# RWKV heads: step outputs formed inside the chain, gathers of the next pair through the levels' banks and ScalarE, ahead of the inversion

## The chip, the cores and the metric

The kernel runs on one core of one Trainium2 chip. The metric is the device time of one execution in microseconds (us); lower is better. The engines of a core are named as in the profile: PE (TensorE; PEld is its weight load), DVE (VectorE), ACT (ScalarE), POOL (GpSimd) and SP (SyncE). PSUM, where PE writes its results, has 8 banks.

## The reference, cut to what matters

The network is two blocks. The first normalises, projects, runs two recurrent mixers side by side (a gated delta rule and RWKV-7) and projects out; the second is banded attention with a conformer convolution. The change touches only the RWKV mixer, which per direction and head is this recurrence over 256 context and 512 latent tokens:

```python
def rwkv7_scan(r, w, k, v, kk, b_vec, s0):
    def step(state, inp):
        r_t, w_t, k_t, v_t, kk_t, b_t = inp
        sa = -jnp.einsum('bhvk,bhk->bhv', state, kk_t)
        state = (state * w_t[:, :, None, :] + sa[..., None] * b_t[:, :, None, :]
                 + v_t[..., None] * k_t[:, :, None, :])
        return state, jnp.einsum('bhvk,bhk->bhv', state, r_t)
    ...

def rwkv_output(o, bonus, z, gn_g, gn_b):
    ...
    y = ((o - mu) * lax.rsqrt(var + GN_EPS)).reshape(b, n, D_RWKV) * gn_g + gn_b
    y = (y + bonus.reshape(b, n, D_RWKV)) * jax.nn.silu(z.astype(jnp.float32))
```

There are 16 heads of 64 channels and two directions; only the outputs of the 512 latent tokens are needed in the end. The two mixers' outputs go through one projection, x + gate * (concat(ya, yb) @ w_out).

## The kernel before, in words

The recurrence is computed in chunks. The 768 tokens are 12 chunks of 64 (4 of context, 8 latent); two heads make a pair, so there are 8 pairs, one after the other, each with both directions at once. For a pair p the stages are these:

- `rwkv_keys(p)` (L932) and in it `rwkv_prep`: loads k and r, forms the decays, A (row operands, rows 12 to 19 of it for the latent outputs) and BK (key operands). `gram` multiplies BK with A on PE into tile `rpg`, and DVE masks it into `Ga` (L1067).
- `rwkv_lanes(p)` (L1072): the inversion of the 64x64 triangles of `Ga`, cut into 32x32 blocks. DVE transposes the blocks into `rL` (L1080), runs 60 operations in a row (`lanes_solve`, L745 and L746, 30 each, tiles `rT` and `rL`), and transposes back.
- `rwkv_rest(p)` (L1091): the second gram, into `Gr` (the masks are DVE again, L1067); copies `R` and the transposes `rpt` that become `bk`; then the gathers for the chain: values (`rpv`, ScalarE copies into `UV`, L1126 and L1127), A transposed (`rat`, L1132, copied into `UV` by DVE, L1133), and Ga times values (`rgv`, L1137, copied into `GS` by ScalarE, L1139). There are 6 each of `rpv`, `rat` and `rgv` in a pair.
- `rwkv_levels(p)` (L1148): puts the 32x32 inverses together (`rpy`, `rpx`), then applies them to what the gathers brought (`rmx`).
- `rwkv_chain(p)` (L1175): the 12 steps that follow one another. A step multiplies Ga with GS (`pU`, L1184), ScalarE copies the result into `UV` (L1186), PE adds the state and bk times UV in the other half of the same bank (L93 is the helper that accumulates), and DVE scales it into the next `GS` (L1195). That last operation is called the state update; there are 11.
- `rwkv_o(p)`: 64 matmuls, after the whole chain, form the outputs from all 12 `UV` and `GS` in tile `rpo`.
- `rwkv_out(p)` (L971): group norm on DVE, transposes back on PE (`rpto`, L993), bonus and gate on GpSimd, and a DMA to `y_scr`.

The banks of PSUM in this phase are four pairs: tag "g" (grams, gathers, prep), tag "l" (the levels), tag "pU" (chain, outputs, output transposes) and "mm" for the filler. `A`, `BK`, `Gr`, `bk`, `R` and `Ga` have two buffers, `UV`, `GS`, `rL` and `rT` one.

What order the instructions stand in is decided by a scheduler that takes what is ready by priority. The work of the pairs stands under `tc.high_priority(offset=4000)`. Beside it runs filler of low priority: large matmuls (`mm`, three products of split operands for each tile) that project the inputs of pair p+2 (`rwkv_proj`, L394) and, once there is none left, the first 13 of 16 rows of the output projection (`out_cols`, L1323). With the latter run the sums for the gates, `awt`: weights are loaded and summed up by DVE (L1254). Filler is paced: each `tick(step, n)` in the pair's work makes n slots behind its last matmul, and `Stream` lets the next filler instruction be issued only after its slot. A pair makes 280 slots.

The order of the calls for a pair is short enough to show:

```python
rwkv_rest(p, now)
nxt = rwkv_keys(p + 1) if p + 1 < npairs else None
rwkv_levels(p, now)
rwkv_chain(p, now)
if nxt:
    rwkv_lanes(p + 1, nxt)
rwkv_o(p, now)
rwkv_out(p, now)
```

Of the kernel before, what the change touches and what calls it, by code (L numbers as in the profile page):

```python
# [10 lines left out]
FT = mybir.dt.float32  # L11
# [7 lines left out]
P = 128  # L19
# [185 lines left out]
def build(tc, a, dbg=None):  # L205
# [5 lines left out]
    with root:  # L211
# [717 lines left out]
        def pg_(shape, name):  # L929
            return gps.tile(shape, FT, name=name, tag="g", bufs=2)  # L930
# [160 lines left out]
        def rwkv_rest(p, s):  # L1091
# [21 lines left out]
            for d in dirs:  # L1113
                rv = (lambda t: t[:, :, ::-1]) if d else (lambda t: t)
                vr = vv
                if d:
                    vr = t3("vr")
                    S.activation(rv(ck(vr)), ck(vv), AF.Copy)
                v00 = rp.tile([P, P], FT, name="v00", tag="wup", bufs=2)
                G.tensor_copy(v00.rearrange("p (o t) -> p o t", o=2), vr[:, 0:64].rearrange("p (o t) -> p o t", o=1).to_broadcast([P, 2, 64]))  # L1120
                for i0 in range(0, NC, 4):
                    pt = pg_([P, 4, P], "rpv")
                    for i in range(4):
                        c = step_chunk[d][i0 + i]
                        w2 = vr[:, 64 * (c - 1):64 * (c + 1)] if c else v00
                        PE.transpose(pt[:, i, :], w2, ident)  # L1126
                    S.activation(UV[64:, i0:i0 + 4, d].rearrange("p i h t -> p i (h t)"), pt[64:], AF.Copy)  # L1127
                for c0 in range(0, NC, 4):
                    i0 = step_chunk[d].index(c0 + (3 if d else 0))
                    pt = pg_([P, 4, P], "rat")  # L1130
                    for c in range(4):
                        PE.transpose(pt[0:64, c, :], A[d][:, c0 + c], ident)  # L1132
                    V.tensor_copy(UV[0:64, c0:c0 + 4, d].rearrange("p c h t -> p c (h t)"), pt[0:64])  # L1133
                    pt = pg_([P, 4, 2, 64], "rgv")
                    for i in range(4):
                        for h in range(2):
                            PE.matmul(pt[halves[h], i, h, :], Ga[64:, d, step_chunk[d][i0 + i], h], UV[64:, i0 + i, d, h, :], start=True, stop=True, skip_group_check=True)  # L1137
                    for h, hp_ in enumerate(halves):
                        S.activation(GS[0:64, i0:i0 + 4, d, h], pt[hp_, :, h], AF.Copy)  # L1139
# [34 lines left out]

        def rwkv_chain(p, s):  # L1175
            mark(f"r{p} chain")
            Ga, UV, GS, bk, WC = (s[n] for n in ("Ga", "UV", "GS", "bk", "WC"))
            flat = lambda t: t.rearrange("p d h t -> p (d h t)")
            for i in range(NC):
                pU = cps.tile([P, 2, 2, 64], FT, name="pU", tag="pU")  # L1180
                for d in dirs:
                    for h in range(2):
                        ks = slice(0, P if i else 64)
                        step = PE.matmul(pU[0:64, d, h], Ga[ks, d, step_chunk[d][i], h], GS[ks, i, d, h], start=True, stop=True, skip_group_check=True)  # L1184
                tick(step, 4)
                S.activation(UV[0:64, i], pU[0:64], AF.Copy)  # L1186
                if i < NC - 1:
                    acc = Acc(tc)
                    if i:
# [4 lines left out]
                    tick(step, 4)  # L1194
                    state = V.tensor_tensor(GS[64:, i + 1], pU[64:], WC[64:, i].rearrange("p d (h o) -> p d h o", o=1).to_broadcast([64, 2, 2, 64]), op=OP.mult)  # L1195
                    states.append(state.ins)

        def rwkv_o(p, s):
            mark(f"r{p} o")
            Gr, R, UV, GS = (s[n] for n in ("Gr", "R", "UV", "GS"))  # L1200

            po = cps.tile([P, 4, 2, 64], FT, name="rpo", tag="pU")
            acc = Acc(tc)
            for part in range(2):
                for d in dirs:
                    for h in range(2):
                        for c in range(4, NC):
                            i = step_chunk[d].index(c)
                            dst = po[halves[c % 2], c // 2 - 2, h]
                            if part == 0:  # L1210
                                step = acc(dst, Gr[d][:, c - 4, h], UV[:, i, d, h, :])
                            else:
                                step = acc(dst, R[d][64:, h, c - 4], GS[64:, i, d, h])
                            if c % 4 == 3:
                                tick(step, 2)
            s["po"] = po

        npairs = {"rwkv": 2}.get(dbg, 8)

# [2 lines left out]
        def tick(step, n):  # L1222

            credit[0] += n
            while credit[0] >= 1:
                slots.append(step.ins)
                credit[0] -= 1
# [55 lines left out]
            rwkv_proj(p, r0, False, pace, tag="mix", bufs=2)  # L1283
        with tc.high_priority(offset=4000):
            now = rwkv_keys(0)
            rwkv_lanes(0, now)
        for p in range(npairs):
            start.append(len(slots))
            with tc.high_priority(offset=4000):
                rwkv_rest(p, now)  # L1290
                nxt = rwkv_keys(p + 1) if p + 1 < npairs else None
                rwkv_levels(p, now)
                rwkv_chain(p, now)
                if nxt:
                    rwkv_lanes(p + 1, nxt)
                rwkv_o(p, now)
                rwkv_out(p, now)
                now = nxt
            beside = Beside()
# [490 lines left out]
```

## Time and profile before

| what | value |
| --- | --- |
| time, median of 3 runs | 3431.95 us (3423.43 to 3436.43) |
| the profiled execution | 3426.15 us, span 3424.3 us |
| granted clock of PE, mean | 0.91 of full |
| PE busy | 3107.4 us, 91% of the span |
| PEld busy | 2464.2 us, 72% |
| DVE busy | 2342.5 us, 68% |
| ACT busy | 1277.3 us, 37% |
| POOL busy | 953.5 us, 28% |

The profile is of one execution. Its span is the time between the first and the last instruction recorded. Busy time is a share of the whole; since the program has stages with different limits, the rows further down are for stretches of it. The pairs' chains lie between about 1300 and 2490 us. The granted clock is the share of full speed that the chip allowed PE; its two levels are 1.2 and 2.4 GHz, and a mean between 0.5 and 1 is a mixture of them. In rows on operations, `out<-in` names the tiles, `x` is a count, and a bracket behind a row holds the idle time of the engine ahead of it and what ended that.

### The profile page before, as it was taken

The page shows a single profiled execution, that of the slowest core. Times are in us where ns is not written, and L with a number is a line of the kernel's source. Part 1 is how long each engine was busy: PE and PEld are TensorE (multiplying, and loading weights), DVE is VectorE, ACT ScalarE, POOL GpSimd, SP SyncE. Part 2 cuts the span into 40 slices and gives each one's busy share as a digit, 9 for nine tenths or more (in the row PEclk, how much of TensorE's full clock was granted, in tenths as well). Part 3 has the DMA queues.
Part 4 walks back from the last instruction along what each step waited for, and adds up shares of the span by engine and source line. Part 5 has one row for each costly group of instructions (what it writes and reads, how often), then busy time and mean ns, then how long its engine had stood idle before and what let it go on. Part 6 is the DMA issues. An engine that isn't in the chain of part 4 may idle for free. (4 is left out here: it accounts for less than half of the span.)

```text
span 3424.3 us, 53583 instructions
## 1 busy us (share of the span) xinstructions
PE 3107.4 (91%) x20464; PEld 2464.2 (72%) x20464; DVE 2342.5 (68%) x4044; ACT 1277.3 (37%) x2719; POOL 953.5 (28%) x794
## 2 busy tenths in 40 slices
PE   7898898999898979999899988898968999999996
PEld 4487787788776767767677766676656778877775
DVE  7977768876786264555636478979358997573577
ACT  4133443344433333334333333331323336574423
POOL 3644344334442323233232325231042000002001
PEclk9899999999998978899798987888878999999998
DMA  8522222222212311112121236575143322223764
GB/s 327 194 75 80 78 78 64 67 78 78 72 63 78 100 56 53 61 57 69 45 73 57 70 91 208 182 234 183 41 164 127 120 86 87 87 80 117 253 214 135
DMA packets 206267, 375.14 MB, mean 110 GB/s; under 512 B 21912, under 2 KB 52281, under 8 KB 202681
## 3 DMA queue, kind: packets, MB, share of 16 engines
q1 hardware_dynamic: 196384, 356.07, 32.4%
q10 hardware_dynamic: 9624, 15.64, 1.3%
q8 instruction: 160, 2.62, 0.3%
q14 instruction: 99, 0.80, 0.1%
HBM read 333.75 MB, written 37.88 MB: 109 GB/s over the span
## 5 line engine op out<-in xcount | busy, mean ns | idle before, releaser
L275 POOL TENSOR_TENSOR w_l<-w_f,w_h 128x512 fp32r<-128x512 f32 x380 | 532.5, 1403 | 1058.5 <-ACT w_h L274 972.2
L274 ACT ACTIVATE w_h<-w_f 128x512 fp32r<-128x512 f32 (+2 forms) x688 | 424.3, 618 | 808.7 <-PE mm L394 277.1
L394 PE MATMUL mm<-hxh,w_h 128*128 128x512 f32 x1472 | 619.9, 421 | 11.9 <-ACT w_h L274 10.8
L394 PE MATMUL mm<-hxh,w_l 128*128 128x512 f32 x1472 | 619.1, 421 | 8.9 <-DVE w_l L275 4.9
L394 PE MATMUL mm<-hxl,w_h 128*128 128x512 f32 x1472 | 609.3, 414 | 0.0
L394 PEld LDWEIGHTS mm<-hxh,w_h 128*128 128x128 f32 x1472 | 289.6, 197 | 73.6 <-ACT w_h L274 13.8
L394 PEld LDWEIGHTS mm<-hxh,w_l 128*128 128x128 f32 x1472 | 291.0, 198 | 70.6 <-DVE w_l L275 9.2
L394 PEld LDWEIGHTS mm<-hxl,w_h 128*128 128x128 f32 x1472 | 290.2, 197 | 61.1 <-issue 1.2
L275 DVE TENSOR_TENSOR w_l<-w_f,w_h 128x512 fp32r<-128x512 f32 (+2 forms) x308 | 219.9, 716 | 142.7 <-ACT w_h L274 140.9
L1254 DVE SCALAR_TENSOR_TENSOR awt<-awt,cacts 128x512 f32<-128x512 f32 x180 | 168.5, 936 | 18.0 <-DMA awt<-in_w_ada 13.5
L1499 DVE SCALAR_TENSOR_TENSOR uc<-up,vecs,uc 128x512 f32<-128x512 f32 x240 | 169.6, 751 | 2.2 <-ACT uc L1497 1.0
L1065 PEld LDWEIGHTS rpg<-A,BK 64*128 64x128 f32 x1280 | 133.3, 229 | 29.5 <-issue 9.9
L394 PE MATMUL mm<-hch,w_l 128*128 128x256 f32 x512 | 153.0, 299 | 1.4 <-POOL w_l L275 1.3
L1065 PE MATMUL rpg<-A,BK 64*128 64x64 f32 x1280 | 142.2, 319 | 13.2 <-POOL BK L1051 6.8
L394 PE MATMUL mm<-hch,w_h 128*128 128x256 f32 x512 | 149.7, 293 | 0.0
L394 PE MATMUL mm<-hcl,w_h 128*128 128x256 f32 x512 | 147.4, 288 | 0.0
L745 DVE TENSOR_TENSOR DG<-L 128x30 f32<-128x30 f32 (+14 forms) x240 | 135.8, 566 | 5.4
L746 DVE TENSOR_TENSOR L<-L,DG 128x30 f32<-128x30 f32 (+14 forms) x240 | 133.7, 557 | 5.4
L1195 DVE TENSOR_TENSOR GS<-pU,WC 64x256 f32<-64x256 f32 x88 | 37.6, 428 | 136.2 <-PE pU L93 131.4
L236 POOL TENSOR_TENSOR cv<-cv,mh 128x4 f32<-128x4 f32 x1 | 1.4, 1437 | 436.8 <-DVE cv L1567 436.8
L745 DVE TENSOR_TENSOR rT<-rL 128x30 f32<-128x30 f32 (+14 forms) x240 | 118.9, 495 | 6.1
L746 DVE TENSOR_TENSOR rL<-rL,rT 128x30 f32<-128x30 f32 (+14 forms) x240 | 116.7, 486 | 6.1
(483 smaller groups left out, 6772.1 us busy)
## 6 DMA issues: line engine op xcount, KB each, us to landing
w_f<-in_w_in SPq DMA_DIRECT2D x496, 256.0 KB, 3.0
awt<-in_w_ada SPq DMA_DIRECT2D x192, 256.0 KB, 3.3
wt<-in_w_ada_t SPq DMA_DIRECT2D x20, 1024.0 KB, 7.1
w_f<-in_w_out SPq DMA_DIRECT2D x80, 256.0 KB, 3.1
awt<-in_w_ada_g SPq DMA_DIRECT2D x64, 256.0 KB, 3.2
wk<-in_w_ada_s SPq DMA_DIRECT2D x16, 768.0 KB, 6.5
w_f<-in_w_out_a SPq DMA_DIRECT2D x48, 256.0 KB, 3.2
lth<-lora_scr SPq DMA_DIRECT2D x32, 288.0 KB, 3.7
```

The costliest lines, as they stand in the source:

```text
L236: G.tensor_tensor(out, in_, mh[:in_.shape[0]].to_broadcast([in_.shape[0], n]), op=OP.pow)
L274: S.activation(wh, raw, AF.Copy)
L275: lower[0].tensor_tensor(wl, raw, wh, op=OP.subtract)
L394: PE.matmul(po[:, :n], w_[:, k, :], h_, start=(kt == 0 and i == 0), stop=(kt == KT - 1 and i == 2))
L745: V.tensor_tensor(t, U[:, r, k:k + 1].to_broadcast([n, k, nc_]), U[:, k:k + 1, c].to_broadcast([n, k, nc_]), op=OP.mult)
L746: step = V.tensor_tensor(U[:, r, c], U[:, r, c], t, op=OP.add)
L1065: ticks[p, d, "gram"] = PE.matmul(pg[h][:, c], BK[hp_, c0 + c, :, :], cols[hp_, c], start=True, stop=True, skip_group_check=True).ins
L1195: state = V.tensor_tensor(GS[64:, i + 1], pU[64:], WC[64:, i].rearrange("p d (h o) -> p d h o", o=1).to_broadcast([64, 2, 2, 64]), op=OP.mult)
L1254: V.scalar_tensor_tensor(wt, wt, cvec[:, k:k + 1], acc, op0=OP.mult, op1=OP.add)
L1499: V.scalar_tensor_tensor(uc[t], up[:, j:j + NX], cw(j), uc[t], op0=OP.mult, op1=OP.add)
```

## The change

Three things are changed in the RWKV part. Line numbers after it shift a little: the chain's `pU` is L1201 and its state update L1214.

1. The gathers. Tiles `rat` and `rgv` are taken from the levels' tag "l" instead of "g", and the copy of `rat` into `UV` is ScalarE's instead of DVE's.
2. The outputs. `rwkv_o` is gone. `outputs(i)` forms what step i adds to the outputs; it is called in step i+1 behind the copy of `UV`, and once after the loop. Its tile `rpo` comes from tag "l" rather than "pU". The tick behind the `pU` matmuls makes 3 slots instead of 4, and the ticks of `rwkv_o` are gone, so that a pair has 236 slots.
3. The inversion of a pair is called after its own `rwkv_rest` and ahead of the next pair's `rwkv_keys`, and no longer behind the chain of the pair before.

```diff
--- before.py
+++ after.py
@@ -1127,11 +1127,11 @@
                     S.activation(UV[64:, i0:i0 + 4, d].rearrange("p i h t -> p i (h t)"), pt[64:], AF.Copy)
                 for c0 in range(0, NC, 4):
                     i0 = step_chunk[d].index(c0 + (3 if d else 0))
-                    pt = pg_([P, 4, P], "rat")
+                    pt = gps.tile([P, 4, P], FT, name="rat", tag="l")
                     for c in range(4):
                         PE.transpose(pt[0:64, c, :], A[d][:, c0 + c], ident)
-                    V.tensor_copy(UV[0:64, c0:c0 + 4, d].rearrange("p c h t -> p c (h t)"), pt[0:64])
-                    pt = pg_([P, 4, 2, 64], "rgv")
+                    S.activation(UV[0:64, c0:c0 + 4, d].rearrange("p c h t -> p c (h t)"), pt[0:64], AF.Copy)
+                    pt = gps.tile([P, 4, 2, 64], FT, name="rgv", tag="l")
                     for i in range(4):
                         for h in range(2):
                             PE.matmul(pt[halves[h], i, h, :], Ga[64:, d, step_chunk[d][i0 + i], h], UV[64:, i0 + i, d, h, :], start=True, stop=True, skip_group_check=True)
@@ -1174,16 +1174,35 @@
 
         def rwkv_chain(p, s):
             mark(f"r{p} chain")
-            Ga, UV, GS, bk, WC = (s[n] for n in ("Ga", "UV", "GS", "bk", "WC"))
+            Ga, UV, GS, bk, WC, Gr, R = (s[n] for n in ("Ga", "UV", "GS", "bk", "WC", "Gr", "R"))
             flat = lambda t: t.rearrange("p d h t -> p (d h t)")
+
+            po = s["po"] = gps.tile([P, 4, 2, 64], FT, name="rpo", tag="l")
+            oacc = Acc(tc)
+
+            def outputs(i):
+
+                for part in range(2):
+                    for d in dirs:
+                        c = step_chunk[d][i]
+                        if c < 4:
+                            continue
+                        for h in range(2):
+                            dst = po[halves[c % 2], c // 2 - 2, h]
+                            if part == 0:
+                                oacc(dst, R[d][64:, h, c - 4], GS[64:, i, d, h])
+                            else:
+                                oacc(dst, Gr[d][:, c - 4, h], UV[:, i, d, h, :])
             for i in range(NC):
                 pU = cps.tile([P, 2, 2, 64], FT, name="pU", tag="pU")
                 for d in dirs:
                     for h in range(2):
                         ks = slice(0, P if i else 64)
                         step = PE.matmul(pU[0:64, d, h], Ga[ks, d, step_chunk[d][i], h], GS[ks, i, d, h], start=True, stop=True, skip_group_check=True)
-                tick(step, 4)
+                tick(step, 3)
                 S.activation(UV[0:64, i], pU[0:64], AF.Copy)
+                if i:
+                    outputs(i - 1)
                 if i < NC - 1:
                     acc = Acc(tc)
                     if i:
@@ -1194,26 +1213,7 @@
                     tick(step, 4)
                     state = V.tensor_tensor(GS[64:, i + 1], pU[64:], WC[64:, i].rearrange("p d (h o) -> p d h o", o=1).to_broadcast([64, 2, 2, 64]), op=OP.mult)
                     states.append(state.ins)
-
-        def rwkv_o(p, s):
-            mark(f"r{p} o")
-            Gr, R, UV, GS = (s[n] for n in ("Gr", "R", "UV", "GS"))
-
-            po = cps.tile([P, 4, 2, 64], FT, name="rpo", tag="pU")
-            acc = Acc(tc)
-            for part in range(2):
-                for d in dirs:
-                    for h in range(2):
-                        for c in range(4, NC):
-                            i = step_chunk[d].index(c)
-                            dst = po[halves[c % 2], c // 2 - 2, h]
-                            if part == 0:
-                                step = acc(dst, Gr[d][:, c - 4, h], UV[:, i, d, h, :])
-                            else:
-                                step = acc(dst, R[d][64:, h, c - 4], GS[64:, i, d, h])
-                            if c % 4 == 3:
-                                tick(step, 2)
-            s["po"] = po
+            outputs(NC - 1)
 
         npairs = {"rwkv": 2}.get(dbg, 8)
 
@@ -1283,17 +1283,14 @@
             rwkv_proj(p, r0, False, pace, tag="mix", bufs=2)
         with tc.high_priority(offset=4000):
             now = rwkv_keys(0)
-            rwkv_lanes(0, now)
         for p in range(npairs):
             start.append(len(slots))
             with tc.high_priority(offset=4000):
                 rwkv_rest(p, now)
+                rwkv_lanes(p, now)
                 nxt = rwkv_keys(p + 1) if p + 1 < npairs else None
                 rwkv_levels(p, now)
                 rwkv_chain(p, now)
-                if nxt:
-                    rwkv_lanes(p + 1, nxt)
-                rwkv_o(p, now)
                 rwkv_out(p, now)
                 now = nxt
             beside = Beside()
```

How the scheduler then orders the instructions is shown in three places. The first is DVE at the end of the third pair's chain, before: `GS<-pU,WC` is a state update, `rL<-Ga` the first transposes of the fourth pair's inversion, `rT`/`rL` its operations, and `mr` belongs to filler.

```order
L1195 TENSOR_TENSOR GS<-pU,WC 64x256 x3
L1141 SCALAR_TENSOR_TENSOR ksum<-rmix,vecs_r,ksum 128x512
L1067 TENSOR_TENSOR Ga<-rpg,consts_r 128x8x64 x2
L1195 TENSOR_TENSOR GS<-pU,WC 64x256
L1080 STREAM_TRANSPOSE rL<-Ga 32x1024 x2
L425 SCALAR_TENSOR_TENSOR mr<-mm,vecs,mr 128x8x63
L1067 TENSOR_TENSOR Ga<-rpg,consts_r 128x4x64 x2
L1080 STREAM_TRANSPOSE rL<-Ga 32x1024 x2
L745 TENSOR_TENSOR rT<-rL 128x30
L746 TENSOR_TENSOR rL<-rL,rT 128x30
L745 TENSOR_TENSOR rT<-rL 128x58
L746 TENSOR_TENSOR rL<-rL,rT 128x29x2
```

And in the changed kernel, where `GS<-pU,WC` is L1214 and six of the eleven updates of this chain stand ahead of these rows:

```order
L1214 TENSOR_TENSOR GS<-pU,WC 64x256
L1067 TENSOR_TENSOR Ga<-rpg,consts_r 128x4x64
L1080 STREAM_TRANSPOSE rL<-Ga 32x1024 x2
L425 SCALAR_TENSOR_TENSOR mv<-mm,vecs,mv 32x448 x2
L425 SCALAR_TENSOR_TENSOR mv<-mm,vecs,mv 64x448
L745 TENSOR_TENSOR rT<-rL 128x30
L746 TENSOR_TENSOR rL<-rL,rT 128x30
L745 TENSOR_TENSOR rT<-rL 128x58
L746 TENSOR_TENSOR rL<-rL,rT 128x29x2
L745 TENSOR_TENSOR rT<-rL 128x84
L746 TENSOR_TENSOR rL<-rL,rT 128x28x3
L745 TENSOR_TENSOR rT<-rL 128x108
```

Before, the last update of the chain stands ahead of all transposes and operations of the inversion. In the changed kernel the transposes stand behind the sixth update, and the next updates stand between the inversion's operations.

The second place is PE, one step of the same chain, before: `mm` is filler, `pU<-GS,consts` adds the state.

```order
L394 MATMUL mm<-hxh_85,w_h 128x512
L394 MATMUL mm<-hxh_85,w_l 128x512
L1184 MATMUL pU<-GS,Ga 64x64 x4
L394 MATMUL mm<-hxl_1050,w_h 128x512
L394 MATMUL mm<-hxh_86,w_h 128x512
L394 MATMUL mm<-hxh_86,w_l 128x512
L394 MATMUL mm<-hxl_1100,w_h 128x512
L93 MATMUL pU<-GS,consts 64x256
L93 MATMUL pU<-UV,bk 64x64 x4
L394 MATMUL mm<-hxh_87,w_h 128x512
L394 MATMUL mm<-hxh_87,w_l 128x512
L394 MATMUL mm<-hxl_1177,w_h 128x512
```

And in the changed kernel:

```order
L394 MATMUL mm<-hxh_79,w_l 128x512
L394 MATMUL mm<-hxl_743,w_h 128x512
L1201 MATMUL pU<-GS,Ga 64x64 x4
L93 MATMUL rpo<-GS,R 64x64 x4
L394 MATMUL mm<-hxh_80,w_h 128x512
L394 MATMUL mm<-hxh_80,w_l 128x512
L394 MATMUL mm<-hxl_788,w_h 128x512
L93 MATMUL pU<-GS,consts 64x256
L93 MATMUL pU<-UV,bk 64x64 x4
L93 MATMUL rpo<-UV,Gr 64x64 x4
L394 MATMUL mm<-hxh_81,w_h 128x512
L394 MATMUL mm<-hxh_81,w_l 128x512
```

The eight output matmuls of the step before stand in two groups of four, behind `pU<-GS,Ga` and behind `pU<-UV,bk`, and one filler less stands in the step.

The third place is PE at the gathers of the fourth pair, before; `rpx` and `rpy` are its levels:

```order
L394 MATMUL mm<-hxh_86,w_h 128x512
L394 MATMUL mm<-hxh_86,w_l 128x512
L394 MATMUL mm<-hxl_1100,w_h 128x512
L394 MATMUL mm<-hxh_87,w_h 128x512
L1132 MATMUL rat<-consts,A 64x128 x4
L1160 MATMUL rpx<-Ga,rL 32x32 x6
L1137 MATMUL rgv<-UV,Ga 64x64 x8
L1160 MATMUL rpx<-Ga,rL 32x32 x9
L1132 MATMUL rat<-consts,A 64x128 x4
L1160 MATMUL rpx<-Ga,rL 32x32
L1155 MATMUL rpy<-rL,Ga 32x32 x16
```

And in the changed kernel, between the third pair's chain and the fourth pair's levels; `rbo` is the bonus:

```order
L394 MATMUL mm<-hxh_78,w_h 128x512
L394 MATMUL mm<-hxh_78,w_l 128x512
L394 MATMUL mm<-hxl_666,w_h 128x512
L1126 MATMUL rpv<-consts,v_15484 128x128
L1126 MATMUL rpv<-consts,vmix 128x128 x11
L1137 MATMUL rgv<-UV,Ga 64x64 x8
L1132 MATMUL rat<-consts,A 64x128 x4
L1126 MATMUL rpv<-consts,vr 128x128 x3
L1126 MATMUL rpv<-consts,v_15557 128x128
L1126 MATMUL rpv<-consts,vr 128x128 x4
L1137 MATMUL rgv<-UV,Ga 64x64 x8
L1132 MATMUL rat<-consts,A 64x128 x4
```

Before, `rat` and `rgv` stand among the levels' matmuls and filler. Now they alternate in a row with `rpv`, ahead of the levels, with no filler between them.

## Rows read from the trace of the kernel before

**Rows 1.** Table of stretches of the span: busy time, clock and DMA

```profile
core 0: us, PE busy (x) PEld busy (x) DVE busy (x) ACT busy (x) POOL busy (x), PEclk, DMA share, GB/s
1308.00:2048.00 740.00, 696.19 (x5997) 531.90 (x5999) 410.41 (x677) 268.10 (x504) 218.22 (x157) 0.88 0.21 63
1598.00:1662.00 64.00, 62.67 (x479) 43.75 (x473) 29.11 (x43) 26.80 (x52) 28.24 (x20) 1.00 0.25 75
1662.00:1744.00 82.00, 74.20 (x713) 60.99 (x713) 50.23 (x96) 26.21 (x49) 11.79 (x9) 0.73 0.16 46
1664.00:1698.00 34.00, 29.93 (x213) 25.87 (x213) 32.17 (x65) 4.90 (x8) 0.00 (x0) 0.50 0.06 16
2048.00:2265.00 217.00, 187.57 (x1357) 142.57 (x1355) 187.56 (x261) 73.58 (x139) 82.43 (x58) 0.77 0.65 202
2265.00:2441.00 176.00, 161.45 (x1297) 124.37 (x1294) 135.19 (x218) 55.13 (x108) 33.43 (x25) 0.90 0.53 166
2441.00:2509.00 68.00, 44.97 (x400) 32.05 (x398) 11.87 (x27) 9.60 (x23) 4.16 (x3) 0.63 0.15 47
```

**Rows 2.** Waits of PE, 1308 to 2048 us: total, count, longest

```profile
PE rpt L1105 <- DVE Gr L1067: 15.1, 5, 4.2
...
PE rpy L1155 <- DVE rL L1084: 5.1, 2, 4.3
```

**Rows 3.** Waits of PE, 2048 to 2509 us

```profile
PE pU L1184 <- DVE GS L1195: 26.5, 18, 4.2
```

**Rows 4.** Groups by line: count | busy us, mean ns | idle before, its causes

```profile
L93 PE MATMUL rpo<-GS,R 64*64 64x64 f32 x512 | 30.4, 269 | 0.0
...
L93 PE MATMUL rpo<-UV,Gr 128*64 128x64 f32 x512 | 25.4, 257 | 0.0
...
L745 DVE TENSOR_TENSOR rT<-rL 128x30 f32<-128x30 f32 (+14 forms) x240 | 118.9, 495 | 6.1
L746 DVE TENSOR_TENSOR rL<-rL,rT 128x30 f32<-128x30 f32 (+14 forms) x240 | 116.7, 486 | 6.1
...
L1133 DVE COPY UV<-rat 64x512 f32<-64x512 f32 x48 | 32.6, 678 | 74.0 <-PE rat L1132 74.0
...
L1127 ACT ACTIVATE UV<-rpv 64x512 f32<-64x512 f32 x48 | 27.7, 591 | 20.2 <-PE rpv L1126 15.2 <-DMA awt<-in_w_ada 4.5
...
L1139 ACT ACTIVATE GS<-rgv 64x256 f32<-64x256 f32 x96 | 36.4, 379 | 51.4 <-PE rgv L1137 50.6
...
L1254 DVE SCALAR_TENSOR_TENSOR awt<-awt,cacts 128x512 f32<-128x512 f32 x180 | 168.5, 936 | 18.0 <-DMA awt<-in_w_ada 13.5 <-DMA awt<-in_w_ada_g 1.7
...
L1195 DVE TENSOR_TENSOR GS<-pU,WC 64x256 f32<-64x256 f32 x88 | 37.6, 428 | 136.2 <-PE pU L93 131.4 <-ACT w_h L274 3.1 <-ACT hxh L1312 0.7
```

**Rows 5.** Timeline of ACT, two steps in a chain: start us, us, instruction

```profile
1618.32 0.38 ACT L1186 ACTIVATE UV<-pU 64x256 f32<-64x256 f32 x1 [0.17 <-PE pU L1184]
...
1622.35 0.38 ACT L1186 ACTIVATE UV<-pU 64x256 f32<-64x256 f32 x1 [2.23 <-PE pU L1184]
```

**Rows 6.** Timeline of PE, two fills in a row

```profile
2214.45 0.40 PE L1323 MATMUL mm<-hxh,w_h 128*128 128x512 f32 x1
2214.69 0.39 PE L1323 MATMUL mm<-hxh,w_l 128*128 128x512 f32 x1
```

**Rows 7.** Timeline of DVE, inversion's start and end, last rat copy

```profile
1658.53 3.90 DVE L1080 STREAM_TRANSPOSE rL<-Ga 32x1024 f32<-32x1024 f32 x2
...
1703.23 0.70 DVE L1089 STREAM_TRANSPOSE rT<-rT 32x512 f32<-32x512 f32 x1
...
1738.65 0.68 DVE L1133 COPY UV<-rat 64x512 f32<-64x512 f32 x1 [2.41 <-PE rat L1132]
```

**Rows 8.** Timeline of DVE and POOL, two steps of an inversion

```profile
1542.01 1.62 DVE L745 TENSOR_TENSOR rT<-rL 128x240 f32<-128x240 f32 x1
1543.67 0.57 DVE L746 TENSOR_TENSOR rL<-rL,rT 128x240 f32<-128x240 f32 x1
...
1540.11 3.10 POOL L275 TENSOR_TENSOR w_l<-w_f,w_h 128x512 fp32r<-128x512 f32 x2
```

**Rows 9.** Timeline of PE, the first large matmul behind the last chain

```profile
2509.25 0.80 PE L1323 MATMUL po<-hxh,w_h 128*128 128x512 f32 x1 [7.34 <-ACT hxh L1312]
```

## The prediction

> **What bounds the kernel now.** I read the table of stretches first, then the waits of TensorE (PE), then the timelines at the edges of a chain. The eight pairs of heads run one after another: a chain of 12 steps, then the inversion and the levels of the next pair, then its chain. Five such periods lie between 1308 and 2048 us, 148 us each [rows 1]. In them PE is busy 696.2 of 740 us: 43.8 us idle, under 9 per period. Its mean granted clock there is 0.88, so 0.12 x 2 of the time, 178 us, ran at the lower of the two levels (1.2 instead of 2.4 GHz). In one period the reader is to see two halves: the chain, 64 us at clock 1.00, and the 82 us up to the next chain at 0.73, with 34 us at 0.50 while VectorE (DVE), busy 32 of them, runs the inversion. So PE starves and slows at the inversion; the chain is fed well. What PE waits for in the five periods is mostly the masks of Gr, queued on DVE among the inversion's steps (15.1 us), and the inversion itself (5.1) [rows 2].
> The last 461 us (2048 to 2509) differ: PE idles 67 us, the clock is 0.77, 0.90 and 0.63 in its three rows, and the last chain has no filler: it and the way from it to the next large matmuls take 68 us, with PE busy 45 [rows 1]. Here the chain's state update comes late, 26.5 us in 18 waits [rows 3], behind the awt sums, which fill DVE (187.6 of 217 us).
>
> **Outputs inside the chain.** The 64 output matmuls of a pair (512 records of each kind over 8 pairs) occupy PE (30.4 + 25.4) / 8 = 7.0 us per pair [rows 4], before and after. A clean step lasts 4.03 us [rows 5] with eight fills in it. A fill follows its predecessor by 0.23 us at the full clock [rows 6], so in each step the eight output matmuls (0.9 us) replace one fill: +0.7 us in 8 or 9 steps, taken from the stage after the chain. Sum: 0. What hides the short ScalarE and DVE waits within a step stays: three or four fills and four output matmuls on each side.
>
> **Fewer slots.** Each tick sets where a filler matmul may stand. With the output stage's ticks gone and three instead of four on half of the chain's, the filler is spread further: in the order, 1055 fillers stand between the ends of the first and the sixth pair's mx stage before, 961 after. So 94 x 0.23 = 21.6 us leave the five periods and come back later. The last chain gets about 118 fillers and the stretch behind it 91.
>
> **Gathers.** Six copies of rat per pair leave DVE (0.68 us each) for ScalarE; the same shape there takes 0.59 [rows 4]. DVE gives up 4.1 us per pair, ScalarE takes on 3.5. In the period before, the last of these copies ran 35 us after the inversion's last instruction [rows 7], within the levels, and mx needs them. After, the gathers stand ahead of the levels in one block on PE, almost without filler: rat and rgv alternate in the two banks of the levels, so each waits for ScalarE's copies of the one before. ScalarE's share is 6 x 0.59 + 6 x 0.59 + 12 x 0.38 = 11.6 us [rows 4]; with six turns of about 0.5 us of hand-over I estimate 15 us, against some 10 us of PE work. That exposes 4 us per period more than now (bounds: 0, if ScalarE runs ahead, and 15, if nothing overlaps). The output tile holds one of these banks through the chain, so the first gather also waits until DVE has read it, which stands earlier in the order than the gathers do.
>
> **The inversion under the chain.** This follows from the order more than from the call's place: the keys of the next pair no longer wait for the old gathers, so its inversion starts about five state updates before the chain's end, and 32 of its 60 DVE operations stand ahead of the last updates. One inversion costs (118.9 + 116.7) / 8 = 29.5 us and its four first transposes 2 x 3.90 = 7.8 [rows 4, 7]. What this takes away: of the 20.2 us in [rows 2] I credit 3 us per period (bounds 0 and 4). What is late next is the second direction's Gr masks, which still have 28 operations of the inversion and the mean and variance ahead of them on DVE. Clock: 178 / 5 = 36 us per period ran at the lower level; on a PE that is bound half of that, 18 us, is loss. I estimate that 79 fillers, now right behind the chain, keep the clock for part of it: 4 us per period (bounds 0 and 12). Price: the DVE queue ahead of a state update holds up to 12 steps of the inversion (0.5 us mean, so 6 us) against a chain step of 4.7 us; two updates per chain slip by about 1 us each: +2 per period (bounds 0 and 13, see the third rival).
> A step of the inversion that ran beside GpSimd took 1.62 us where its twin took 0.57 [rows 8], and GpSimd is busy 28.24 us in a chain of 64 and not at all in the 34 us where the inversion runs now [rows 1]. If 32 steps meet it in 0.44 of the time, 14 x 1.05 = 15 us of DVE work are added, of which the slack of the chain (35 us of DVE idle) takes most; that is in the +2. The Trainium skill (GPSIMD Engine Reference, 1. Specifications) says that GpSimd's ports to SBUF are shared with VectorE, and contended by instructions with two SBUF inputs, as these are; by it the move costs DVE time in every period, and with a third of the 15 us on the path the sum would be 3 us per period higher, 3385.
>
> **Sum.** First stretch, five periods: -21.6 (fillers moved) - 15 (waits) - 20 (clock) + 20 (gathers) + 10 (updates) = -26.6 us. Last stretch: +21.6 (the same fillers). The last chain and what follows take 68 us; their own PE work is 12 x (4.03 - 8 x 0.23) = 26 plus 7 of outputs, so 35 us are free; fillers use them, less 5 us of new waits: -30. This includes the 7.3 us ahead of the next large matmuls [rows 9], which 39 fillers (9 us) now cover. The awt sums (168.5 us of DVE [rows 4]) move from pairs 5 to 7 into 6 and 7, with 50 of them beside one chain and its whole inversion (about 100 us of DVE, some 90 us of PE): +10; but the stretch of 217 us loses load: of the 44 us idle up to 2441 I take 22 off. Together -12. Clock there: -10 of at most 49.9 + 17.6 + 25.2 = 93 (the missing shares of [rows 1]; bounds 0 and 93; nearest, the clock term above). Last stretch: -30.4. Start and pair 0: 0 (bounds -5 and +5). In all -57. The profiled execution took 3426.15 us (span 3424.3), 5.8 below the median 3431.95 of the three runs. 3426 - 57 = 3369; with that offset 3375; I say 3370. Within 0.5%, 17 us, I call it no change: runs of this kernel spread over 13 us.
>
> **Rivals.**
> 1. Larger gain: gathers and updates hide entirely (-30 in the first stretch) and the clock returns 8 us per period instead of 4 (-20): 3320. For it: PE's named waits are few, and the inversion's 34 us are the slow part of the period. Against it: PE idles only 43.8 us in the five periods, and part of that are hand-overs that stay.
> 2. The gain is eaten on PE. The waits removed return in the gather block, and the clock falls there instead of at the inversion: its 10 us of small matmuls take 5 us more, in seven periods 35: 3405. For it: PE is 94% busy in the five periods, and small matmuls with waits between them are what ran at 0.50 [rows 1]. The Trainium skill (Perfetto Trace Analysis, Matmul Optimizations) says that the matmul engine scales its power with use and wants matmuls back to back in batches; the trace agrees with 1.00 in the filled chain against 0.50 in the inversion, and by that rule a block without filler is the wrong place for the gathers. Against it: most of the filler behind the chain stands ahead of that block.
> 3. Slower: the inversion moves onto the chain's path. It, its transposes and six updates of 0.43 are 29.5 + 7.8 + 2.6 = 40 us of DVE [rows 4, 7] beside six steps of 64 / 12 = 5.3 (32 us): 8 us over, and 5 more by five stretched steps beside GpSimd. If the keys come late, as the masks of Ga wait for GpSimd's products, all of it falls on the last updates: +13 us per period instead of +2. Seven periods give +77; the clock gain goes too (+20): 3370 + 97 = 3467. It decides if the first transpose of an inversion starts after the eighth of the 11 updates of a chain. For it: DVE takes its work in order, and 26.5 us of just this wait stand where awt sums were queued [rows 3]. Against it: in the chain DVE was busy 29 of 64 us [rows 1], so there is room for 20 us more.
> 4. Nothing of it shows: the outputs' 7 us and the fillers only change places: 3426.
>
> **How the numbers follow.** Forecast 0.38, rival 1 0.20, rival 2 0.22, rival 3 0.13, rival 4 0.07. Faster (under 3415): 0.38 + 0.20 + 0.6 x 0.22 = 0.71. Same: 0.4 x 0.22 + 0.07 = 0.16. Slower: 0.13. The range reaches from rival 1 with more of its clock bound (25 less) to a little past no change: 3295 to 3440; rival 3 and larger gains are left out. The forecast's own range is 3340 to 3400.
>
> **What would show it.** Right: the five periods shrink from 148 to about 143 us; the inversion's last operations come within 20 us of the last update, and the way to the next chain has a clock over 0.80 against 0.73 now; the chain stays under 70 us; the last chain has PE near full, and no gap of 7 us before the first large matmuls behind it. Wrong: state updates that wait for DVE by more than 5 us per chain, PE waits for ScalarE at rgv and rat of more than 6 us per pair, or a first stretch as long as now.

## The result and the profile after

The changed kernel takes 3384.26 us (median of 4 runs, 3375.71 to 3404.72) against 3427.69 before: ratio 0.9864, interval 0.9832 to 0.9895. Timed again later beside other kernels it was 0.9908 (0.9876 to 0.9940). It is faster by about 1%, as forecast (3370; range 3295 to 3440). The profiled execution took 3378.85 us. First the page's head:

```profile
span 3377.1 us, 53576 instructions
...
PE 3093.9 (92%) x20464; PEld 2447.9 (72%) x20464; DVE 2324.4 (69%) x3996; ACT 1303.7 (39%) x2767; POOL 952.6 (28%) x794
```

The table of stretches, as in [rows 1]. The first row is the same five periods, from the first pair's first step to the sixth pair's; the second the rest up to the next large matmuls; then one chain and the way to the next; the gather block inside that; the seventh chain; the last chain; and what follows it.

```profile
core 0: us, PE busy (x) PEld busy (x) DVE busy (x) ACT busy (x) POOL busy (x), PEclk, DMA share, GB/s
1315.40:2021.40 706.00, 672.83 (x5930) 501.45 (x5928) 402.86 (x658) 290.49 (x545) 210.85 (x154) 0.92 0.20 60
2021.40:2462.50 441.10, 395.10 (x3079) 302.32 (x3077) 326.33 (x477) 139.06 (x269) 125.52 (x89) 0.87 0.58 182
1582.90:1650.40 67.50, 65.55 (x541) 46.32 (x536) 43.24 (x70) 18.64 (x38) 18.84 (x14) 0.95 0.16 52
1650.40:1719.50 69.10, 64.18 (x648) 50.59 (x650) 37.29 (x64) 38.06 (x69) 22.68 (x16) 0.95 0.24 71
1683.00:1700.00 17.00, 16.82 (x184) 13.00 (x183) 3.07 (x7) 12.77 (x27) 1.27 (x1) 0.92 0.38 108
2161.20:2279.10 117.90, 101.36 (x675) 77.10 (x676) 99.51 (x151) 28.51 (x57) 35.24 (x27) 0.83 0.52 158
2366.80:2437.00 70.20, 64.86 (x501) 47.04 (x501) 46.98 (x74) 14.23 (x32) 3.43 (x3) 1.00 0.67 211
2437.00:2457.00 20.00, 19.92 (x95) 15.78 (x94) 7.65 (x14) 6.69 (x12) 4.23 (x3) 1.00 0.45 140
```

The five periods take 706.0 instead of 740 us, the rest 441.1 instead of 461. For the pair shown, the way to the next chain has clock 0.95 where it had 0.73, now that the inversion is gone from it; the chain pays for that with 0.95 against 1.00 and 3.5 us. Over the five pairs the ways shrink from 400 to 357 us in all and the chains grow from 340 to 349. The last chain, which was not quite empty before (18 fillers, by the trace), has 145 at clock 1.00. Not in the table: the first chain starts 7.4 us later (1315.4 against 1308.0). So -34.2, -20.0 and +7.4 make the 47 us between the spans.

On DVE the first transposes of the fourth pair's inversion now stand in the third pair's chain (L1214 is its state update), and the inversion ends 19 us behind that chain's last step at 1650.4 (21 behind its last update):

```profile
1617.79 3.88 DVE L1080 STREAM_TRANSPOSE rL<-Ga 32x1024 f32<-32x1024 f32 x2
1621.69 0.42 DVE L1067 TENSOR_TENSOR Ga<-rpg,consts_r 128x256 f32<-128x256 f32 x1
1622.15 0.43 DVE L1214 TENSOR_TENSOR GS<-pU,WC 64x256 f32<-64x256 f32 x1
...
1669.44 0.20 DVE L746 TENSOR_TENSOR rL<-rL,rT 128x30 f32<-128x30 f32 x1
```

PE's waits in the five periods, which answer to [rows 2] (total, count, longest):

```profile
PE rpt L1105 <- DVE Gr L1067: 9.6, 8, 1.8
PE pU L1201 <- DVE GS L1214: 6.2, 6, 3.9
PE mm L394 <- POOL w_l L275: 6.0, 4, 1.6
```

The wait for the inversion (5.1) is gone, that for the Gr masks is 9.6 instead of 15.1. PE's idle time fell from 43.8 to 33.2 us. No wait for ScalarE stands at `rat` or `rgv`. The gather block on PE shows why:

```profile
1686.26 0.66 PE L1126 MATMUL rpv<-consts,vmix 128*128 128x128 f32 x4 [0.18 <-ACT UV L1127]
1686.85 0.68 PE L1137 MATMUL rgv<-UV,Ga 64*64 64x64 f32 x16
1687.46 0.63 PE L1132 MATMUL rat<-consts,A 128*64 128x128 f32 x4
...
1698.22 0.68 PE L1137 MATMUL rgv<-UV,Ga 64*64 64x64 f32 x16
```

A `rgv` and a `rat` stand there every 2 to 3 us, other small matmuls between them, and PE is busy 16.8 of 17.0 us: ScalarE keeps up. The end of the last chain, which answers to [rows 9], is an idle time of 3.34 instead of 7.34 us, 13 us behind the output transposes with filler between:

```profile
2449.29 0.60 PE L993 MATMUL rpto<-consts,oa 128*128 128x128 f32 x4
...
2462.46 0.91 PE L1320 MATMUL po<-hxh,w_h 128*128 128x512 f32 x2 [3.34 <-ACT w_h L274]
```

### The profile page after: what moved, and what is told of

The parts are those of the page before. It is cut to its first block, busy times and chain, and to the rows that moved or that the text cites. A ratio compares the mean times of both kernels' runs of the same rounds, so it can differ in the third digit from the quotient of the medians.

```text
span 3377.1 us, 53576 instructions
## 1 busy us (share of the span) xinstructions
PE 3093.9 (92%) x20464; PEld 2447.9 (72%) x20464; DVE 2324.4 (69%) x3996; ACT 1303.7 (39%) x2767; POOL 952.6 (28%) x794
## 4 chain that ended last, share of the span: by engine, by line
PE 55%; DVE 27%; issue 6%; DMA 3%; ACT 2%; POOL 1%; SPq 0%; DVEq 0%; POOLq 0%; ACTq 0%
PE mm L394 24%; PE po L1758 4%; PE mm L1477 4%; DVE L L746 3%; DVE DG L745 3%; PE rpg L1065 3%; DVE awt L1254 2%; DVE rT L745 2%; DVE rL L746 2%; PE pU L93 2%; DVE acc L587 2%; DMA awt<-in_w_ada 2%; DVE uc L1496 2%; PE mm L1320 2%; PE pl L1016 1%
## 5 line engine op out<-in xcount | busy, mean ns | idle before, releaser
L1203 ACT ACTIVATE UV<-pU 64x256 f32<-64x256 f32 x96 | 36.2, 377 | 235.0 <-PE pU L1201 223.9
```

## The experiments

Times are ratios to the kernel before, on the same chip, with the interval; "fillers" are the `mm` matmuls counted in the trace. Stretches come from one profiled execution each: "first" is from the first pair's first step to the sixth pair's, "last" from there to the next large matmuls.

| kernel | ratio (interval) | median us | first, us (fillers) | last, us (fillers) |
| --- | --- | --- | --- | --- |
| before | 1 | 3427.69 | 740.2 (1065) | 461.1 (624) |
| changed: 1, 2 and 3 | 0.9864 (0.9832 to 0.9895) | 3384.26 | 706.0 (966) | 441.1 (728) |
| e7, the same again | 0.9908 (0.9876 to 0.9940) | 3400.34 | 719.8 (966) | 440.7 (727) |
| e1: 1 alone | 1.0084 (1.0056 to 1.0112) | 3452.28 | 771.9 (1101) | 452.2 (591) |
| e2: 2 alone | 1.0020 (1.0002 to 1.0038) | 3434.30 | 712.9 (904) | 494.1 (786) |
| e3: 3 alone | 1.0015 (0.9995 to 1.0035) | 3431.89 | 722.4 (1065) | 479.3 (624) |
| e4: 1 and 2 | 0.9815 (0.9798 to 0.9832) | 3363.61 | 689.9 (903) | 450.3 (789) |
| e10: 1 and 2 again | 0.9774 (0.9739 to 0.9809) | 3348.26 | 690.9 (903) | 454.1 (789) |
| e5: before, pace 1.0 | 0.9976 (0.9952 to 1.0000) | 3417.55 | 748.3 (1065) | 460.5 (624) |
| e6: 1, pace 1.0 | 0.9970 (0.9947 to 0.9993) | 3413.59 | 772.5 (1101) | 409.0 (591) |
| e8: 1 and 2, pace 2.0 | 0.9881 (0.9842 to 0.9921) | 3384.13 | 690.8 (902) | 478.0 (789) |
| e9: 1, slots of 2 | 0.9905 (0.9871 to 0.9940) | 3396.44 | 698.7 (903) | 480.0 (789) |
| e11: 1 and 2, tick 4 | 0.9866 (0.9825 to 0.9907) | 3383.83 | 685.7 (942) | 461.7 (749) |
| e12: 1 and 2, rat on DVE | 0.9871 (0.9836 to 0.9906) | 3381.57 | 676.7 (906) | 469.4 (789) |

**e1 to e3: each part by itself.** e1 takes the three lines of the gathers from the diff, e2 the output lines, e3 the three moved calls.

> Part 1 of the change alone on the kernel before (rat and rgv in the levels' banks, rat copied by ScalarE); outputs and call order as before. In its order the first transposes of an inversion stand behind the 6th (later 3rd and 2nd) of the 11 state updates, as in the changed kernel, but the last chain has no filler at all (47 before, 182 in the changed kernel). My theory (the inversion under the chain gives the first stretch, filler in the last chain the last one): first five periods 15 us shorter, last stretch +5, in all 3410 to 3420, ratio 0.996. Rival A (the outputs inside the chain and the slots they free do it all; the inversion's place gives nothing): no change or slower by the emptier last chain, 3428 to 3440. Rival B (the gathers' place alone gives nearly all, by the clock): 3385 to 3395.

> Part 2 alone on the kernel before: outputs formed in the chain's next step, rpo in the levels' banks, 3 slots instead of 4; gathers and call order as before. In the order the inversion stands behind 6 to 11 updates (11 in every second pair), the last chain has 203 fillers and 187 stand behind it. My theory: the last stretch gains its 20 us or a little more, the first five periods lose only the moved fillers (22 us, given back later): 3400 to 3410, ratio 0.994. Rival A (this part does it all): 3380 to 3390. Rival B (the gathers' place gives nearly all): 3425 to 3435.

> Part 3 alone on the kernel before: the inversion is called behind its own pair's rest and ahead of the next pair's keys; gathers and outputs as before. In the order the inversion still stands behind 7 to 11 updates (10 in most pairs), the last chain has 52 fillers. All theories: no change, 3420 to 3436; if it is faster by more than 10 us, the call's place matters by more than the order of the inversion against the updates shows.

No part alone is faster. e2 lies in rival B's range, but rival B gives nearly all to the gathers, and e1 is 0.8% slower; only its rival A had room for a loss, and less of one (to 3440). In e1 the inversion stands under each chain, as meant. Its five periods, and their waits:

```profile
1313.50:2085.40 771.90, 726.16 (x6089) 547.52 (x6088) 439.27 (x693) 302.42 (x563) 240.46 (x174) 0.87 0.24 77
```

```profile
PE pU L1184 <- DVE GS L1195: 21.2, 9, 7.7
PE rpt L1105 <- DVE Gr L1067: 7.6, 4, 2.2
```

The wait for the Gr masks falls as in the changed kernel, but PE now waits 21.2 us for state updates, which are queued among the inversion's steps, where it waited 6.1; PE's idle time is 45.7 us against 43.8 before and the clock 0.87 against 0.88, so nothing is gained by it. In e2 the inversion lies under only every second chain, and the ways between chains alternate:

```profile
1386.40:1445.80 59.40, 56.99 (x570) 46.20 (x571) 27.11 (x48) 27.33 (x51) 14.78 (x11) 0.89 0.17 55
1507.30:1600.10 92.80, 82.33 (x716) 63.76 (x718) 63.70 (x111) 34.32 (x62) 20.77 (x15) 0.74 0.17 53
1676.50:1728.80 52.30, 50.50 (x557) 40.58 (x558) 22.93 (x36) 26.77 (x50) 14.28 (x11) 0.93 0.22 65
1795.80:1887.00 91.20, 74.61 (x679) 57.44 (x679) 66.47 (x109) 34.03 (x61) 19.02 (x13) 0.81 0.18 54
```

52 to 59 us where it lies under the chain, 91 to 93 where it lies behind. So part 1 is what brings the inversion under each chain, as the prediction read from the order; part 2 does not.

**e4, e10 and e7: two parts together.**

```diff
 with tc.high_priority(offset=4000):
     now = rwkv_keys(0)
+    rwkv_lanes(0, now)
...
-                rwkv_lanes(p, now)
                 nxt = rwkv_keys(p + 1) if p + 1 < npairs else None
                 rwkv_levels(p, now)
                 rwkv_chain(p, now)
+                if nxt:
+                    rwkv_lanes(p + 1, nxt)
```

> Parts 1 and 2 without part 3 (the inversion is called behind the chain of the pair before, as in the kernel before). Order: transposes behind the 6th update, 36 to 52 operations ahead of the last update (35 in the changed kernel), 166 fillers in the last chain and 187 behind it. My theory: as the changed kernel, 3378 to 3394, since the order of DVE is nearly the same; the pair 0 start (7 us later in the changed kernel) is given back, so rather the lower end. Rival (the call order is what lets the gathers pass): 3400 to 3415.

> The changed kernel as it is, timed beside the others on one chip. 3376 to 3392. If it is within 6 us of parts 1 and 2 without 3 (3364), the call order is worth nothing; if the 20 us between them stand, the call's place costs that.

> Parts 1 and 2 without 3 again (e4), beside the others on one chip. 3358 to 3375. If it comes out at 3385 or more, the 20 us to the changed kernel are the spread between chips and executions, and the call's place is worth nothing.

All three medians fell outside what was expected (e4 and e10 below, e7 above). Parts 1 and 2 are the version that beats both kernels, 0.9815 and 0.9774; e10's interval is clear of the changed kernel's two, e4's touches the first of them. Apart they cost 0.8% and 0.2%, together they save 2%. Part 3, which has no term of its own in the sum and is worth nothing alone (e3), costs about 0.5 to 1.3% beside them. The traces place this only in part. In the five periods the changed kernel is 15 us longer than e10 (29 in e7's trace), with 63 more fillers; its chains are 22 us shorter in all and the ways between them 37 longer. The largest piece of that is the levels of the sixth pair, 41.1 us instead of 19.7 a pair earlier, at clock 0.63, behind a wait of PE. The instructions are as many, but 48 instead of 32 `rpg` and 9 instead of 2 `pl`, which belong to the next pair's keys, are among them:

```profile
1839.60:1859.30 19.70, 19.70 (x323) 15.59 (x323) 9.70 (x14) 9.97 (x18) 9.27 (x6) 1.00 0.13 39
1980.30:2021.40 41.10, 38.48 (x327) 28.47 (x326) 14.59 (x21) 16.67 (x32) 12.46 (x10) 0.63 0.08 25
```

```profile
1985.19 1.25 PE L1160 MATMUL rpx<-Ga,rL 32*32 32x32 f32 x29 [2.62 <-ACT rL L1157]
```

The way from the fifth chain to the sixth takes 92.1 us there and 92.2 in e7, but 69.4 in e10. The keys of the seventh pair stand in that place; that part 3 costs its time through them is only argued.

**e5, e6 and e8: the filler's pace alone.** One number, `stream.rate = 1.6`, is 1.0 in e5 and e6 and 2.0 in e8; the order up to the sixth chain stays as it is.

> The kernel before with one number changed: the pace of the out-projection's filler, stream.rate 1.6 to 1.0. The order up to the sixth pair's chain stays as it is; pair 6's chain gets 118 fillers instead of 286, the last chain 115 instead of 47, and 52 stand behind it. My theory now (most of the change's gain in the last stretch is filler that reaches the last chain, where PE had nothing to do): the last stretch 30 us shorter, 3390 to 3402, ratio 0.990. Rival (the filler helps only with the inversion under the chain, as each part alone was no faster): 3422 to 3435, no change.

> The gathers alone (part 1, which took 3452) with stream.rate 1.0: the last chain gets 115 fillers instead of none, 52 stand behind it, and the sixth chain 132 instead of 208. My theory: its last stretch comes back by 45 us, 3400 to 3412; what is then left to the parts 1 and 2 together (3364) is the outputs inside the chain, some 40 us in eight pairs. Rival A (the outputs are worth nothing, as predicted, and the filler is all): 3364 to 3375. Rival B (the gathers' block itself costs, in each pair, and filler can't mend it): 3440 or more.

> Parts 1 and 2 without 3, with stream.rate 2.0: 234 fillers in the last chain instead of 166 and 78 behind it instead of 187. My theory (the last chain is full at 166, PE busy 64.4 of 65.4 us, so more filler only lengthens it): 3357 to 3370, no change to the 3364 of rate 1.6. Rival (filler behind the chain is the cost, 109 fillers of 0.23 us, 25 us): 3335 to 3345.

e5 gains 10 us instead of 30, at the edge of the noise, and in its trace the last stretch is no shorter (460.5 against 461.1): filler in the last chain is not by itself worth what I had credited. In e6 it is worth 39 (3452 to 3414), all of it in the last stretch (452.2 to 409.0 with the same 591 fillers), as its two theories had it for that step; what is left to 1 and 2 together was put at some 40 us and came out at 50 to 65. e8 is 20 us or more slower than e4, against both of its theories. Its seventh chain takes 116.0 us instead of 84.4, with 182 instead of 147 fillers. But the order on DVE changed there too: 60 instead of 28 operations of the next inversion stand ahead of the chain's last update. The two can't be told apart in e8. Runs with about as few fillers in that chain as e4 speak for the inversion, though each differs in one thing more: 85.4 us with 28 operations ahead (e10, 147 fillers), 97.5 with 44 (e12, 145) and 102.8 with 51 (e9, 139). These are the seventh chains of e8 and e9:

```profile
2166.60:2282.60 116.00, 56.66 (x182) 37.28 (x180) 0.00 (x0) 2.38 (x4) 0.81 0.47 148
2183.80:2286.60 102.80, 44.04 (x139) 27.75 (x139) 0.00 (x0) 2.37 (x4) 0.83 0.53 165
```

Their busy times and counts are those of the fillers alone.

**e9: the outputs' place.** Part 1 with the slots of part 2, the outputs behind the chain and in the chain's banks as before:

```diff
-                tick(step, 4)
+                tick(step, 3)
                 S.activation(UV[0:64, i], pU[0:64], AF.Copy)
...
                                 step = acc(dst, R[d][64:, h, c - 4], GS[64:, i, d, h])
-                            if c % 4 == 3:
-                                tick(step, 2)
```

> Parts 1 and 2 without 3 as in e4 (3364), but with the 64 output matmuls of a pair in one block behind the chain, as in the kernel before, and without slots of their own; the filler stands in the same numbers in each chain and between them as in e4 (104, 72, ..., 166, 187). So only the place of the outputs differs. My theory now (in a chain with the inversion under it the outputs fit into PE's gaps, behind it they cost PE their 7 us per pair): first five periods 30 to 37 us longer than e4's 690, in all 3405 to 3425. Rival (as predicted, the place of the outputs is worth nothing on a bound PE, the slots are all): 3360 to 3375.

e9 is 48 us slower than e10 on the same chip, so the place of the outputs (and with it their bank) is worth something, and the rival that follows the prediction's zero falls. But in the five periods it is only 8 us by the traces (698.7 against 690.9), not 30 to 37; 26 lie in the last stretch, where the order on DVE differs too. How much of that is PE's gaps and how much the order is open. The other use of e9 is beside e1: in the code only the slots differ. 198 fillers leave the first stretch, which shrinks by 73.2 us, 0.37 each, and come back in the last, which grows by 27.8, 0.14 each. Of the 73.2 us, 55 and 153 of the fillers lie on the ways between chains, not in the chains. At 0.23 each the fillers make 46 us; PE's idle time is 11 us less (45.7 to 34.3), and the rest goes with the clock (0.87 to 0.88). Both prices come from single traces, whose pieces differ by some 14 us between executions. These two rows of a table of stretches are e9's, all work and its fillers alone:

```profile
1315.90:2014.60 698.70, 664.38 (x5845) 499.29 (x5845) 392.37 (x649) 280.19 (x525) 196.54 (x145) 0.88 0.19 58
...
1315.90:2014.60 698.70, 290.25 (x903) 175.26 (x903) 16.17 (x23) 12.57 (x19) 0.88 0.19 58
```

**e11 and e12.** `tick(step, 4)` in the chain of e4; and e4 with the copies of `rat` on VectorE (`V.tensor_copy`).

> Parts 1 and 2 without 3 with 4 instead of 3 slots behind the U matmuls: 115 fillers per chain instead of 104, 184 in the last chain and 67 behind it instead of 187. My theory (filler that is moved costs the same wherever PE is full): first five periods 15 us longer, the rest 15 shorter, in all 3360 to 3378. Rival (more filler in the chain pushes the steps apart): 3380 to 3395. Rival (less behind the last chain gains): 3340 to 3352.

> Parts 1 and 2 without 3 with the copies of rat on VectorE as before, the tiles still in the levels' banks; filler in the same numbers. As predicted, ScalarE's copies would pace the gathers by 4 us per period: then DVE's copies (4.1 us per pair) would make the gathers shorter but hold up the inversion; net -10 to +10, 3354 to 3375. Rival (the gathers are paced by PE alone, 15.7 us with no wait in e4's trace): no difference beyond 5 us. Rival (DVE copies queue behind the next pair's work): slower by 20 us or more.

Both are about 1% slower than e10, 33 to 36 us by the medians. For e11 the first rival has the number, but its reason is not shown: the seventh chain takes 120.4 us with 183 fillers against 85.4 with 147 in e10, and again 60 instead of 28 operations of the inversion are ahead of its last update. Its five periods, with 39 more fillers than e10's, are not longer (685.7 against 690.9), which goes against the 0.37 of e1 and e9. For e12 the medians speak for the copies on ScalarE, but the traces don't show where: its five periods are shorter than e10's (676.7), its last stretch longer, and its profiled execution is its fastest run while e10's is its slowest. That stays open.

## Why the prediction came out right, and where it was wrong

The forecast of 3370 was 14 us off, its sum of -57 against -47 in the traces. By stretches: start 0 against +7.4 (outside its bounds of 5; without part 3 it is +7.3 in e4 and +4.4 in e10), first -26.6 against -34.2 (-20.4 in e7's trace), last -30.4 against -20.0.

That the total came so close is in part luck. The terms that did come in the first stretch add up to some 66 us: 10.6 of waits, 32 of clock and 99 fillers at 0.23, 23. The stretch shrank by 34.2. Some 30 us stand against them that no wait names (in e7 as well: 51 and 20.4). The sum had +30 there, for gathers and updates, and neither shows in the traces. Part of the 30 is work that moved in from behind: 16 more `rpg` and 16 more `pl` stand in the stretch than before. The rest is open; the clock's share may also be counted too high, since much of the low clock before lay in the inversion, where PE had only 213 matmuls in 34 us [rows 1].

- **Inversion under the chain:** right, and read from the order; it is the gathers' banks that do it (e1). The three signs named for it came out at their bounds over the five pairs: the last operations 18 to 22 us behind the last update (20 was said), the ways at clock 0.95 to 0.97 but the fifth at 0.80 (over 0.80 was said), the chains 68 to 73 us (under 70 was said). The waits gave 10.6 us of idle time, 15 predicted; the clock's loss, (1 - 0.88) x 740 = 89 us, is 0.08 x 706 = 56, 32 less (17 less in e7), 20 predicted.
- **Updates, +2 per period:** in the changed kernel the named wait did not grow (6.1 to 6.2 us), but in e1 it grew by 15 us, 3 per period. Rival 3's mechanism is real, at that size. It can't alone have made e1 a loss, and it is not the thinner filler that kept it small: with the filler thinned, the five periods have 14.8 us of it in e9, and e10, the fastest of all, has 17.0:

```profile
PE pU L1201 <- DVE GS L1214: 17.0, 14, 5.2
```

e10 lacks only part 3, and with it the wait is small (6.2 us, in e7 too). The order goes with that: 31 to 35 operations of the inversion stand ahead of a chain's last update in the changed kernel's five periods, 31 to 48 in e10's and 29 to 50 in e1's. That the order is the reason is argued.

- **Gathers, +20:** wrong. PE waited 0.2 us there; the block runs at PE's own pace, 16.8 us busy of 17.0, clock 0.92. The sum's 10 us of PE work and its 0.5 us of hand-over in a turn are estimates that no row shows.
- **Fewer slots: the step that failed.** "94 x 0.23 = 21.6 us leave the five periods and come back later" has the count right (1065 to 966), but the transfer is not worth zero. Thinning the slots turns part 1 from 0.8% slower to 1% faster (e1, e9). There a filler is worth 0.37 in the first stretch and 0.14 in the last; at these prices 99 of them would be 37 us out and 14 back, not 22 each. That estimate does not carry over everywhere: in e11 39 more fillers did not lengthen the first stretch. The 0.37 holds lost clock and waits, and can't be added to the terms above.
- **Outputs: 0.** Also wrong by its place: 48 us between e9 and e10, of which the traces place 8 in the five periods.
- **Last stretch:** right that the last chain fills (clock 1.00, PE 64.9 of 70.2 us) and that most of the idle time behind it goes (3.3 of 7.3 us stay). That filling it gives 30 us by itself is not shown: e5 fills it and its last stretch is as long as before, in e6 the same pace gives 43. The prediction also takes the last chain before for one without filler, where 18 stand. The awt sums beside a whole inversion were foreseen, but not that the seventh chain would take 117.9 us. Two updates in a row on DVE there:

```profile
2205.55 0.43 DVE L1214 TENSOR_TENSOR GS<-pU,WC 64x256 f32<-64x256 f32 x1
2206.01 3.91 DVE L1080 STREAM_TRANSPOSE rL<-Ga 32x1024 f32<-32x1024 f32 x2
...
2220.53 0.43 DVE L1214 TENSOR_TENSOR GS<-pU,WC 64x256 f32<-64x256 f32 x1
```

15 us for one step, DVE busy 99.5 of 117.9: the +10 set for this, over some 90 us of PE work, was too low. In e10 that chain takes 85.4, with 28 instead of 60 of the inversion's operations ahead of its last update and 147 instead of 187 fillers:

```profile
2159.70:2245.10 85.40, 83.23 (x627) 61.51 (x627) 71.92 (x110) 22.91 (x50) 28.60 (x24) 0.94 0.60 191
```

- **GpSimd beside the inversion, up to 15 us of DVE:** wrong in size. Over eight inversions the two groups of [rows 4] grew from 235.6 to 241.6 us, 0.75 us per inversion. The Trainium skill (GPSIMD Engine Reference, 1. Specifications) names contention for these ports. The sums neither bear out nor refute that it grew with the move: they are 234.8 us in e1, where the inversion stands under the chains, and 250.6 in e3, where it does not. It decides nothing here. These are the changed kernel's rows:

```profile
L745 DVE TENSOR_TENSOR rT<-rL 128x30 f32<-128x30 f32 (+14 forms) x240 | 124.4, 518 | 6.7
L746 DVE TENSOR_TENSOR rL<-rL,rT 128x30 f32<-128x30 f32 (+14 forms) x240 | 117.2, 489 | 6.7
```

Rival 2 fell with the gathers' term: the block of small matmuls without filler kept a clock of 0.92, with 0.2 us of waits in it.

## What to carry to other kernels

Filler is not worth the same everywhere: count how many low-priority instructions each stretch holds before and after, and price them by the stretch they leave and the one they reach, from runs of your own kernel. A change of several parts is not the sum of its parts; here 1 and 2 cost 0.8% and 0.2% alone and save 2% together, and the third takes a part of it away. When serial work is moved under another engine's chain, count how much of it stands ahead of the chain's last step: in the seventh chain here 28 to 51 operations went with 85 to 103 us at about the same filler.

## What was not expected of the hardware

Executions of one program differ by about 1%, and the time goes with PE's mean granted clock: the changed kernel's runs were 3375.71 us at 0.926, 3378.85 at 0.924, 3389.68 at 0.921 and 3404.72 at 0.917. The 29 us between the ends are 0.009 of clock, and 0.009 x 3390 = 31 us. So pieces of single traces are sure to some 14 us only, as the two profiles of the changed kernel show (706.0 and 719.8). Nor does a longer wait have to stand ahead of such a fall. The changed kernel's fourth chain takes 69.9 us at 0.90 in one profile and 76.1 at 0.82 in the other, with the same 0.9 us of waits of PE in it:

```profile
1719.50:1789.40 69.90, 69.01 (x541) 48.87 (x536) 41.70 (x68) 18.62 (x37) 18.52 (x14) 0.90 0.16 50
1735.80:1811.90 76.10, 75.23 (x547) 53.85 (x544) 41.63 (x67) 18.63 (x38) 18.45 (x14) 0.82 0.14 45
```
